# Stick-breaking attention in a two-layer trunk: the short query blocks of two neighbouring pairs of heads computed as one unit

## The chip, the cores and the metric

The kernel runs on one core of one Trainium2 chip. The metric is device time in microseconds (us), from the start of the program to its end. A core has five engines with queues of their own: TensorE (PE), VectorE (DVE), ScalarE (ACT), GpSimd (POOL) and SyncE (SP, which here only starts transfers). Each runs its instructions in the order in which the program has them and waits on semaphores for the others. Matmuls write PSUM, which has eight banks of 512 float32 columns; DVE and ACT read them from there.

## What is computed

One inference step of a decoder trunk with two layers. Layer 0 mixes tokens with a convolution, layer 1 with stick-breaking attention; a gated FFN follows each. There are 512 prompt tokens and 8 x 4 decode tokens with 256 cached keys each. The change touches only the prompt's part of the attention of layer 1:

```
z = einsum('bqhd,bkhd->bhqk', q, k) * HEAD_DIM ** -0.5 + bias      # 16 heads of 64
valid = k_pos < q_pos
log_fail = where(valid, log_sigmoid(-z), 0)
after = cumsum(log_fail, reverse=True) - log_fail
weights = where(valid, exp(log_sigmoid(z) + after), 0)
out = einsum('bhqk,bkhd->bqhd', weights, v)                        # then out @ attn_w_o
```

Queries go in blocks of 128; block i sees the first (i + 1) x 128 keys.

## The kernel before, in words

**Heads and units.** The 16 heads are 8 pairs (`pair(c)`, L2206); the two heads of a pair lie in the two halves of the 128 partitions. A pair's four query blocks need 512, 384, 256 and 128 keys. They are cut into three units (`UNITS`, L2202): block 3 (512 columns), blocks 2 and 0 side by side (384 + 128 = 512 columns), and block 1 (256 columns).

**Steps of a unit** (`unit`, L2210). PE computes the logits of both heads into two PSUM banks (L2221, tag `z`). ACT takes the exponential of each (L2226) into a tile `e`. POOL clears what is not causal (L2233). DVE clamps (L2238). ACT takes the logarithm of 1 + e into a tile `s` (L2240). DVE sums it from the right with a scan for each head and block (L2249). ACT takes exp(-s) (L2253). DVE multiplies e by it (L2254): these are the weights. PE transposes them in squares of 128 (L2261) into the one bank with tag `t`, a head at a time, and ACT copies each head's transposes into a tile `w` (L2264). PE then multiplies them with the values (`products`, L2277) into the one bank with tag `av`.

**Tiles.** There are three `e` and three `w` tiles of 2 x 512 columns, one of each with 2 x 256, and one `s` tile of each size (L80). An `e` tile is free when it is transposed, a `w` tile when its products are done.

**After a pair.** For the first seven pairs ACT copies the result over the pair's queries (L2292); its split into a high and a low part (`XH` by ACT, L2286, and `XL` by DVE, L2287, in `out`) is held out until the last pair is planned. For the last pair the split reads the bank `av` itself, in four pieces of 128 columns.

**Work beside it.** In the same stage PE projects keys and values of all pairs, with float32r matmuls in threes (`weighted`, L1981 to L1983: high x high, high x low, low x high), each operation being six matmuls over two of the eight input chunks. They are the fill. The decode tokens' logits and products (L2101, L2163, L2183) and transposes of pages, keys and values (L2089, L2011) are in between. At the end of the stage the fill is the first four output products (attention result times `attn_w_o`, L2345), into banks `acc`, `z`, `z` and `one`. Each is four operations; the last of each four needs the last two pairs' `XH` and `XL`.

**What sets the order.** Each step is given to a planner (`Plan`, L85) with an engine, an estimated cost, and what it reads and writes. `run` (L170) goes through time: for each engine it takes the ready operation with the lowest key, which is its start less a share of its rank (the longest chain behind it) less `urgent`. `fill` operations come after all others that are ready within 0.15. A matmul of another array shape (`form`: logits use 64 rows, products 64 columns, the decode products 32 columns) than the one before is charged 0.17. The instructions are issued in this order.

**After the stage.** DVE adds the four banks to the residual `xT` (L2361), in the order `acc`, `z`, `z`, `one`. PE goes on with `add_group` (L2368): the same four weight slots for the other 288 token columns, in new banks (L460 to L462). The first of these takes the PSUM bank in which the `acc` product lay, so its first matmul waits for the first add.

Of the kernel before, what the change touches and what calls it, by code (L numbers as in the profile page):

```python
# [13 lines left out]
AF = mybir.ActivationFunctionType  # L14
# [3 lines left out]
P = 128  # L18
# [58 lines left out]

BIG = 1.0e17
AHEAD = 3
E_BUFS, S_BUFS, W_BUFS = (3, 1), (1, 1), (3, 1)  # L80
NEAR, PATIENT = 0.15, 2.0


# [142 lines left out]
def tile_trunk(  # L226
# [207 lines left out]
    def uid(s):  # L434
        _n[0] += 1
        return f"{s}_{_n[0]}"
# [197 lines left out]
    start_cm, start = open_pool("start")  # L634
# [42 lines left out]
    plan = Plan(E_CONV, 0.12)  # L677
# [382 lines left out]
    for c in range(0, NC, 2):  # L1060
# [137 lines left out]
    for h, (c0, n) in enumerate(STREAMS):  # L1198
        if h:
            layer_norm(1)  # L1200
        for g in (0, 4):
            for i in range(4):
                c = g + i
                pt = product(s0 + c, h)
                x = xT[:, c, c0:c0 + n]
# [3 lines left out]
        if not h:  # L1209
# [6 lines left out]
    n = SA[1]  # L1216
    plan.op("pe", 0.53, lambda: pe.matmul(ms()[:, :n], mean_m, nrm.acc[0]()[:, :n], start=True, stop=True),
            r=[nrm.acc[0]], w=[ms])
    plan.op("act", 0.34, lambda: act.activation(rs()[:, :n], ms()[:, :n], AF.Sqrt, bias=eps_t[:, 0:1], scale=1.0),
            r=[ms, "table"], w=[rs])  # L1220
    plan.op("dve", 1.7, lambda: dve.reciprocal(rs()[:, :n], rs()[:, :n]), w=[rs])
    for c in range(NC):
        u = plan.tile("u", NC, lambda: nrm.tile("u", NC))
        e, name, cost = on("pool" if c in POOL_U else "dve", n, 1.05e-3, 2.25e-3)
        plan.op(name, cost, lambda c=c, u=u, e=e: e.tensor_tensor(u()[:, :n], xT[:, c, 0:n], rs()[:, :n], op=ALU.mult),
                r=[rs, ("x", c, 0)], w=[u])
# [4 lines left out]
            r=[u, ("XH", c, 0)], w=[("XL", c, 0)], lift=NLIFT)  # L1231
# [694 lines left out]
    HALF = [slice(0, HD), slice(HD, P)]  # L1926
# [5 lines left out]
    plan = Plan()  # L1932
# [14 lines left out]
    def sbuf(tag, w, bufs, dt=F32, pool_=va):  # L1947
        return plan.tile(tag, bufs, lambda: pool_.tile([P, w], dt, tag=tag, name=uid(tag), bufs=bufs))
# [7 lines left out]
    def dcost(n):  # L1956
        return 0.09 + n * 1.1e-3

    def acost(n):
        return 0.1 + n * 0.95e-3  # L1960
# [238 lines left out]
            r=[t], w=["Zd0", "Zd1"] + [("Zd", i) for i in range(4)])  # L2199


    UNITS = [[(3, 0)], [(2, 0), (0, 3 * P)], [(1, 0)]]  # L2202

    held_out = []

    def pair(c):  # L2206
        b = [bb[:, 2 * c + j:2 * c + j + 1] for j in range(2)]
        av = psum("av")

        def unit(u, parts):  # L2210
            n = sum((i + 1) * P for i, _ in parts)
            z = [psum("z") for _ in range(2)]
            e, s, w = (sbuf(f"{tag}{n}", 2 * n, bufs[n < 512]) for tag, bufs in (("e", E_BUFS), ("s", S_BUFS), ("w", W_BUFS)))

            def two(x):
                return x()[:, :2 * n].rearrange("p (j k) -> p j k", j=2)

            def logits():
                for i, lo in parts:
                    for j in range(2):  # L2220
                        pe.matmul(z[j]()[:, lo:lo + (i + 1) * P], qT[HALF[j], c, i * P:(i + 1) * P],  # L2221
                                  kT[HALF[j], c, 0:(i + 1) * P], start=(lo == 0), stop=True, skip_group_check=True)

            plan.op("pe", 1.69e-3 * n, logits, r=[("q", c), ("k", c, 0), ("k", c, 1)], w=z, form="r64")
            for j in range(2):
                plan.op("act", acost(n), lambda j=j: act.activation(two(e)[:, j, :n], z[j]()[:, :n], AF.Exp, bias=b[j]),  # L2226
                        r=[z[j]], w=[(e, j)])


            def causal():  # L2230
                for i, lo in parts:
# [8 lines left out]
            plan.op("act", acost(2 * n), lambda: act.activation(two(s)[:, :, :n], two(e)[:, :, :n], AF.Ln, bias=1.0),  # L2240
                    r=ej, w=[(s, 0), (s, 1)])

            for j in range(2):
                for i, lo in parts:
# [9 lines left out]
            plan.op("dve", 0.08 + 2 * n * 1.08e-3, lambda: dve.tensor_tensor(  # L2254
                two(e)[:, :, :n], two(e)[:, :, :n], two(s)[:, :, :n], op=ALU.mult), r=sj, w=ej)
            for j in range(2):
                t = psum("t")

                def turn(j=j, t=t):
                    for k in range(n // P):  # L2260
                        pe.transpose(t()[:, k * P:(k + 1) * P], two(e)[:, j, k * P:(k + 1) * P], ident)  # L2261

                plan.op("pe", 0.82e-3 * n, turn, r=[(e, j)], w=[t])
                plan.op("act", acost(n), lambda j=j, t=t: act.copy(two(w)[:, j, :n], t()[:, :n]), r=[t], w=[(w, j)])  # L2264

            return w

        ws = [unit(u, parts) for u, parts in enumerate(UNITS)]

        def products(us, cost, key):  # L2270
            def f():
                for u in us:
                    w = ws[u]
                    for i, lo in UNITS[u]:
                        for kc in range(i + 1):
                            for j in range(2):
                                pe.matmul(av()[HALF[j], i * P:(i + 1) * P], vtok[c % 3][:, kc, HALF[j]],  # L2277
                                          w().rearrange("p (j k) -> p j k", j=2)[:, j, lo + kc * P:lo + (kc + 1) * P],
                                          start=(kc == 0), stop=(kc == i), skip_group_check=True)

            plan.op("pe", cost, f, form="c64", w=[key],
                    r=[*((ws[u], j) for u in us for j in range(2)), ("vtok", c % 3, 0), ("vtok", c % 3, 1)])

        def out(lo, n, src, r, key):
            cols = slice(lo, lo + n)
            plan.op("act", acost(n), lambda: act.copy(XH[:, c, cols], src(cols)), r=r, w=[("XH", c, key)], a=[("X", c)])  # L2286
            plan.op("dve", dcost(n), lambda: dve.tensor_tensor(XL[:, c, cols], src(cols), XH[:, c, cols], op=ALU.subtract),  # L2287
                    r=[*r, ("XH", c, key)], a=[("X", c)])

        if c < NC - 1:  # L2290
            products(range(len(UNITS)), 2.1, av)
            plan.op("act", acost(512), lambda: act.copy(qT[:, c, 0:SEQ], av()), r=[av], w=[("q", c)])  # L2292
            held_out.append(lambda: out(0, SEQ, lambda cols: qT[:, c, cols], [("q", c)], 0))
        else:
            for u in range(len(UNITS)):
                products([u], 0.82e-3 * 2 * sum((i + 1) * P for i, _ in UNITS[u]), (av, u))
            for u in range(len(UNITS)):
                for i, _ in UNITS[u]:
                    out(i * P, P, lambda cols: av()[:, cols], [(av, u)], i)

    def both_halves(f, c):
# [37 lines left out]
    for i, tag in enumerate(("acc", "z", "z", "one")):  # L2339
# [66 lines left out]
```

## Time and profile before

| | |
|---|---|
| median of the runs (lowest, highest) | 1284.79 us (1284.37, 1285.92) |
| profiled execution: its own time | 1284.92 us |
| profiled execution: span | 1283.2 us |
| PE busy in the span | 1267.9 us (99%) |
| DVE busy, ACT busy, POOL busy | 979.9, 713.7, 152.9 us |
| TensorE clock granted, mean | 0.998 |

The span is the time from the first to the last instruction that the profiler recorded; the execution's own time is 1.7 us more. A row of the timeline has the start and the duration of an instruction, both in us, then engine, line, operation, and output <- inputs with their shapes. A number in brackets is the time that the engine sat idle before it, and what ended that. PE overlaps its matmuls: a matmul of 128 x 256 has a row of some 0.28 us, but the next one starts 0.12 us later. So PE is "busy" in the records even where it does less than it can, and what a step takes is read from the distance between starts. [...]

### The profile page before, as it was taken

The numbers are of one execution on the slowest core, as the hardware profiler recorded it, in microseconds if no ns is written. First come the engines' busy times: TensorE is split into PE (matmuls) and PEld (weight loads), VectorE is DVE, ScalarE is ACT, GpSimd is POOL, SyncE is SP. The second block draws the span as 40 slices with busy tenths as digits, with TensorE's granted clock in tenths as the row PEclk, the third lists the DMA queues.
The fourth block names the chain that finished last, engine by engine and source line by source line (L and its number), as shares of the span: only waits on it lengthen the run. The fifth ranks groups of instructions, "written<-read, shape, count | busy, mean of one in ns | idle before, by whom it ended". The sixth has DMA issues, their size and how long they took to land.

```text
span 1283.2 us, 26496 instructions
## 1 busy us (share of the span) xinstructions
PE 1267.9 (99%) x10860; PEld 1213.6 (95%) x10860; DVE 979.9 (76%) x1671; ACT 713.7 (56%) x1440; POOL 152.9 (12%) x289
## 2 busy tenths in 40 slices
PE   9999999999999999999999999999999999999997
PEld 8997799999999999999988988889999999999997
DVE  6899876988987887768366586756988987886864
ACT  7596574645654455445356587754645555454453
POOL 4000014111001000000142123100111011000000
PEclk9999999999999999999999999999999999999999
DMA  8465333123233233144543445333132233232221
GB/s 223 121 181 136 88 100 115 34 84 115 91 108 101 78 106 116 59 142 138 180 152 128 140 133 174 110 117 99 50 101 87 95 117 115 67 111 90 90 76 70
DMA packets 119402, 142.38 MB, mean 111 GB/s; under 512 B 5357, under 2 KB 110469, under 8 KB 119010
## 3 DMA queue, kind: packets, MB, share of 16 engines
q1 hardware_dynamic: 110350, 111.89, 28.2%
q0 software_dynamic: 8640, 28.78, 7.0%
q8 instruction: 85, 1.39, 0.5%
q14 instruction: 35, 0.29, 0.1%
q10 hardware_dynamic: 292, 0.02, 0.0%
HBM read 129.34 MB, written 12.18 MB: 110 GB/s over the span
## 4 chain that ended last, share of the span: by engine, by line
PE 84%; DVE 11%; issue 2%; ACT 1%; DMA 1%; DVEq 0%; SPq 0%; POOL 0%; ACTq 0%; POOLq 0%
PE acc L1557 5%; PE acc L1555 5%; PE acc L1556 5%; PE acc L712 4%; PE acc L713 4%; PE acc L714 3%; PE acc L460 3%; PE acc L462 3%; PE acc L461 3%; PE tr L1557 3%; PE tr L1556 3%; PE tr L1555 3%; PE av L1353 3%; PE acc L1981 3%; PE av L1355 3%; PE av L1354 3%
## 5 line engine op out<-in xcount | busy, mean ns | idle before, releaser
L373 DVE TENSOR_TENSOR wlo<-raw,whi 128x1024 fp32r<-128x1024 f32 (+2 forms) x245 | 257.4, 1052 | 45.5 <-ACT whi L370 43.8
L370 ACT CAST whi<-raw 128x1024 fp32r<-128x1024 f32 (+2 forms) x245 | 223.5, 914 | 117.3 <-PE av L1354 24.6
L712 PE MATMUL acc<-XH,whi 128*128 128x288 f32 (+1 forms) x384 | 114.5, 298 | 0.0
L713 PE MATMUL acc<-XL,whi 128*128 128x288 f32 (+1 forms) x384 | 110.9, 289 | 0.1
L714 PE MATMUL acc<-XH,wlo 128*128 128x288 f32 (+1 forms) x384 | 110.4, 288 | 0.1
L1981 PE MATMUL acc<-XH,whi 128*128 128x256 f32 (+1 forms) x264 | 82.8, 314 | 0.6 <-ACT XH L2286 0.6
L1555 PE MATMUL acc<-TH,whi 128*128 128x272 f32 x288 | 82.9, 288 | 0.0
L1557 PE MATMUL acc<-TH,wlo 128*128 128x272 f32 x288 | 82.8, 288 | 0.0
L1556 PE MATMUL acc<-TL,whi 128*128 128x272 f32 x288 | 82.8, 287 | 0.0
L1591 ACT COPY G<-acc 128x272 f32<-128x272 f32 (+1 forms) x72 | 26.8, 372 | 94.9 <-PE acc L1557 94.9
L1353 PE MATMUL av<-HH,whi 128*128 128x288 f32 x256 | 76.2, 298 | 0.2
L1982 PE MATMUL acc<-XL,whi 128*128 128x256 f32 (+1 forms) x264 | 76.2, 289 | 0.1
L1983 PE MATMUL acc<-XH,wlo 128*128 128x256 f32 (+1 forms) x264 | 75.9, 287 | 0.0
L1354 PE MATMUL av<-HL,whi 128*128 128x288 f32 x256 | 75.5, 295 | 0.0
L1355 PE MATMUL av<-HH,wlo 128*128 128x288 f32 x256 | 75.3, 294 | 0.0
L712 PEld LDWEIGHTS acc<-XH,whi 128*128 128x128 f32 x384 | 72.2, 188 | 2.8 <-issue 1.6
L713 PEld LDWEIGHTS acc<-XL,whi 128*128 128x128 f32 x384 | 72.3, 188 | 1.0 <-DVE XL L964 0.3
L714 PEld LDWEIGHTS acc<-XH,wlo 128*128 128x128 f32 x384 | 72.2, 188 | 0.3 <-DVE wlo L373 0.3
L1354 PE MATMUL tr<-HL,whi 128*128 128x256 f32 x256 | 71.9, 281 | 0.0
L1353 PE MATMUL tr<-HH,whi 128*128 128x256 f32 x256 | 71.9, 281 | 0.0
L1355 PE MATMUL tr<-HH,wlo 128*128 128x256 f32 x256 | 71.5, 279 | 0.0
L1494 DVE SCALAR_TENSOR_TENSOR cv<-G,fprm,cv 128x560 f32<-128x560 f32 x88 | 69.4, 797 | 0.5
(405 smaller groups left out, 4391.8 us busy)
## 6 DMA issues: line engine op xcount, KB each, us to landing
raw<-in_ffn_w_gate_dram SPq DMA_DIRECT2D x22, 1024.0 KB
raw<-in_ffn_w_up_dram SPq DMA_DIRECT2D x22, 1024.0 KB
raw<-in_ffn_w_down_dram SPq DMA_DIRECT2D x24, 768.0 KB
raw<-in_attn_w_qkv_dram SPq DMA_DIRECT2D x12, 1024.0 KB
raw<-in_conv_w_in_dram POOLq DMA_DIRECT2D x6, 1024.0 KB, 7.9
rep<-glu SPq DMA_DIRECT2D x36, 142.0 KB
raw<-in_conv_w_out_dram POOLq DMA_DIRECT2D x4, 1024.0 KB, 5.8
raw<-in_ffn_w_down_dram SPq DMA_DIRECT2D x8, 512.0 KB
```

The lines of the kernel that those rows point to most:

```text
L370: act.copy(hi[:, k, :], src[:, k])
L373: dve.tensor_tensor(lo[:, k, :], src[:, k], hi[:, k, :], op=ALU.subtract)
L712: pe.matmul(o, hi[:, k, :], XH[:, k, c0:c0 + n], start=(k == 0), stop=False)
L713: pe.matmul(o, hi[:, k, :], XL[:, k, c0:c0 + n], start=False, stop=False)
L714: pe.matmul(o, lo[:, k, :], XH[:, k, c0:c0 + n], start=False, stop=(k == NC - 1))
L1353: pe.matmul(o, hi[:, j + k, :], xh, start=(start and k == 0), stop=False, **kw)
L1354: pe.matmul(o, hi[:, j + k, :], xl, start=False, stop=False, **kw)
L1355: pe.matmul(o, lo[:, j + k, :], xh, start=False, stop=(stop and k == len(xs) - 1), **kw)
L1555: pe.matmul(o, hi[:, j + k, :], xh, start=(start and k == 0), stop=False, **kw)
L1556: pe.matmul(o, hi[:, j + k, :], xl, start=False, stop=False, **kw)
L1557: pe.matmul(o, lo[:, j + k, :], xh, start=False, stop=(k == 3), **kw)
L1981: pe.matmul(o, hi[:, k, :], XH[:, k, c0:c0 + n], start=(k == 0), stop=False)
```

## The change

- Block 1 of pairs c and c + 1 (c even) is one unit of 256 + 256 = 512 columns; it is planned with pair c. There are 4 such units in place of 8 with 256 columns, so 20 units in place of 24. Its two exponentials of each head stay apart, since each pair has its own bias, and so do the scans. Clamp, logarithm, exp(-s), multiplication, and the transposes and copy of each head run over 512 columns of each head.
- The copy after the transposes writes back into `e`; the tiles `w` are gone. There are six `e` and two `s` tiles, all of one size. An `e` tile is now held until its products are done.
- The last pair's three products get `urgent` 3.0, where they had none.

```diff
+LAST_AV = 3.0
-E_BUFS, S_BUFS, W_BUFS = (3, 1), (1, 1), (3, 1)
+E_BUFS, S_BUFS = 6, 2
...
-    UNITS = [[(3, 0)], [(2, 0), (0, 3 * P)], [(1, 0)]]
+    UNITS = [[(3, 0)], [(2, 0), (0, 3 * P)]]
+    shared = {}
...
-                plan.op("act", acost(n), lambda j=j: act.activation(two(e)[:, j, :n], z[j]()[:, :n], AF.Exp, bias=b[j]),
-                        r=[z[j]], w=[(e, j)])
+                for cc, (lo, m) in cs.items():
+                    plan.op("act", acost(m), lambda j=j, cc=cc, lo=lo, m=m: act.activation(
+                        two(e)[:, j, lo:lo + m], z[j]()[:, lo:lo + m], AF.Exp, bias=bb[:, 2 * cc + j:2 * cc + j + 1]),
+                            r=[z[j]], w=[(e, j)])
...
-                plan.op("act", acost(n), lambda j=j, t=t: act.copy(two(w)[:, j, :n], t()[:, :n]), r=[t], w=[(w, j)])
-
-            return w
...
+                plan.op("act", acost(n), lambda j=j, t=t: act.copy(two(e)[:, j, :n], t()[:, :n]), r=[t], w=[(e, j)])
+
+            return e
+
+        ws = [unit([(i, lo, c) for i, lo in parts]) for parts in UNITS]
+        if c % 2 == 0:
+            shared[c] = shared[c + 1] = unit([(1, 0, c), (1, 2 * P, c + 1)])
+        ws.append(shared[c])
+        units = [*UNITS, [(1, c % 2 * 2 * P)]]
...
-                products([u], 0.82e-3 * 2 * sum((i + 1) * P for i, _ in UNITS[u]), (av, u))
+                products([u], 0.82e-3 * 2 * sum((i + 1) * P for i, _ in units[u]), (av, u), LAST_AV)
```

The code is five lines longer at L2223 and eleven at L2361, so lines differ: logits L2221 are L2226 after, transposes L2261 are L2268, the copy L2264 is L2271, products L2277 are L2288, the fill L1981 to L1983 is L1982 to L1984, the splits L2286 and L2287 are L2297 and L2298, the adds L2361 are L2372, and L460 is L461.

**How PE's order moves.** Three places matter below. The first is the last pair's products on PE, before. `z`, `acc` and `one` are banks of output products, `av` is the bank of the last pair, `w` are its transposed weights:

```order
L1983 MATMUL z_10551<-XH,wlo_10231 128x256
L2277 MATMUL av_10643<-w_772_10425,vtok_8050 64x128 x8
L2277 MATMUL av_10643<-w_781_10502,vtok_8050 64x128 x8
L2277 MATMUL av_10643<-w_790_10559,vtok_8050 64x128 x4
L1981 MATMUL acc_10531<-XH,whi_9907 128x256
L1982 MATMUL acc_10531<-XL,whi_9907 128x256
L1983 MATMUL acc_10531<-XH,wlo_9908 128x256
```

Behind the products stand 24 matmuls of fill, four operations of six, and all four of them need the last pair's split; ahead of them stand 36 that do not need it.

The same place after, `e` being the tiles that now hold the weights:

```order
L1984 MATMUL z_10495<-XH,wlo_10148 128x256
L2288 MATMUL av_10506<-e_10270,vtok_8050 64x128 x8
L2288 MATMUL av_10506<-e_10336,vtok_8050 64x128 x8
L2288 MATMUL av_10506<-e_10200,vtok_8050 64x128 x4
L2189 MATMUL one_10534<-ident,oacc 128x128 x2
L1982 MATMUL acc_10469<-XH,whi_9830 128x256
L1983 MATMUL acc_10469<-XL,whi_9830 128x256
L1984 MATMUL acc_10469<-XH,wlo_9831 128x256
```

The products have moved ahead: behind them stand 78 matmuls of fill, 6 ahead of them since the last transposes. The first 33 of the 78 need no split of the last pair.

The second place is the end of the stage on PE, before, where the next stage begins with L460:

```order
L1981 MATMUL one_10618<-XH,whi_10386 128x256
L1982 MATMUL one_10618<-XL,whi_10386 128x256
L1983 MATMUL one_10618<-XH,wlo_10387 128x256
L460 MATMUL acc_10729<-XH,whi_9907 128x288
L461 MATMUL acc_10729<-XL,whi_9907 128x288
```

The product that ends last before is `one`; `acc` was the first of the four to end, 18 matmuls earlier.

And after:

```order
L1984 MATMUL z_10495<-XH,wlo_10148 128x256
L1982 MATMUL acc_10469<-XH,whi_9830 128x256
L1983 MATMUL acc_10469<-XL,whi_9830 128x256
L1984 MATMUL acc_10469<-XH,wlo_9831 128x256
L461 MATMUL acc_10657<-XH,whi_9830 128x288
```

Now `acc` ends last, right ahead of the next stage's first matmul, which writes into the same bank.

The third place is a shared unit's logits, after, on PE; the two numbers are the two heads' banks:

```order
L2226 MATMUL z_10177<-kT,qT 128x256
L2226 MATMUL z_10179<-kT,qT 128x256
L2226 MATMUL z_10177<-kT,qT 128x256
L2226 MATMUL z_10179<-kT,qT 128x256
L2120 MATMUL one_10183<-kT_s,Qf 32x32 x16
```

Before, each pair's two such matmuls stand as a group of their own, at eight places; now four stand together, at four places.

More of the change, by code (lines that the diff above doesn't have):

```diff
@@ L2199, in new_values, with unit @@
             r=[t], w=["Zd0", "Zd1"] + [("Zd", i) for i in range(4)])
-    UNITS = [[(3, 0)], [(2, 0), (0, 3 * P)], [(1, 0)]]
+    UNITS = [[(3, 0)], [(2, 0), (0, 3 * P)]]
+    shared = {}
     held_out = []
     def pair(c):
-        b = [bb[:, 2 * c + j:2 * c + j + 1] for j in range(2)]
         av = psum("av")
-        def unit(u, parts):
-            n = sum((i + 1) * P for i, _ in parts)
+        def unit(parts):
+            n = 512
             z = [psum("z") for _ in range(2)]
-            e, s, w = (sbuf(f"{tag}{n}", 2 * n, bufs[n < 512]) for tag, bufs in (("e", E_BUFS), ("s", S_BUFS), ("w", W_BUFS)))
+            e, s = (sbuf(tag, 2 * n, bufs) for tag, bufs in (("e", E_BUFS), ("s", S_BUFS)))
+            cs = {}
+            for i, lo, cc in parts:
+                a, m = cs.get(cc, (lo, 0))
+                cs[cc] = (a, m + (i + 1) * P)
             def two(x):
@@ L2243, in unit @@
             for j in range(2):
-                for i, lo in parts:
+                for i, lo, _ in parts:
                     m = (i + 1) * P
@@ L2263, in unit, with products @@
                 plan.op("pe", 0.82e-3 * n, turn, r=[(e, j)], w=[t])
-                plan.op("act", acost(n), lambda j=j, t=t: act.copy(two(w)[:, j, :n], t()[:, :n]), r=[t], w=[(w, j)])
-            return w
-        ws = [unit(u, parts) for u, parts in enumerate(UNITS)]
-        def products(us, cost, key):
+                plan.op("act", acost(n), lambda j=j, t=t: act.copy(two(e)[:, j, :n], t()[:, :n]), r=[t], w=[(e, j)])
[5 more added lines that the diff above has]
+        units = [*UNITS, [(1, c % 2 * 2 * P)]]
+        def products(us, cost, key, urgent=0.0):
             def f():
@@ L2273, in f @@
                     w = ws[u]
-                    for i, lo in UNITS[u]:
+                    for i, lo in units[u]:
                         for kc in range(i + 1):
@@ L2279, in f @@
                                           start=(kc == 0), stop=(kc == i), skip_group_check=True)
-            plan.op("pe", cost, f, form="c64", w=[key],
+            plan.op("pe", cost, f, form="c64", w=[key], urgent=urgent,
                     r=[*((ws[u], j) for u in us for j in range(2)), ("vtok", c % 3, 0), ("vtok", c % 3, 1)])
@@ L2290, in pair @@
         if c < NC - 1:
-            products(range(len(UNITS)), 2.1, av)
+            products(range(len(units)), 2.1, av)
             plan.op("act", acost(512), lambda: act.copy(qT[:, c, 0:SEQ], av()), r=[av], w=[("q", c)])
@@ L2294, in pair @@
         else:
-            for u in range(len(UNITS)):
-                products([u], 0.82e-3 * 2 * sum((i + 1) * P for i, _ in UNITS[u]), (av, u))
-            for u in range(len(UNITS)):
-                for i, _ in UNITS[u]:
+            for u in range(len(units)):
+                products([u], 0.82e-3 * 2 * sum((i + 1) * P for i, _ in units[u]), (av, u), LAST_AV)
+            for u in range(len(units)):
+                for i, _ in units[u]:
                     out(i * P, P, lambda cols: av()[:, cols], [(av, u)], i)
```

10 lines of the change are left out of this document (5 added, 5 removed).

## The prediction

> **What bounds the kernel now.** I read the page first: 26496 instructions, PE busy nearly everywhere. Then the busy times of the attention stage (start of its first fill matmul to the first L460) beside a stretch behind it that is nothing but back-to-back fill:
>
> ```profile
> span 1283.2 us, 26496 instructions
> 642.83:859.40 216.57, 214.77 (x2111) 187.40 (x2110) 147.41 (x228) 145.88 (x274) 51.85 (x71) 1.00 0.44 141
> 860.00:872.00 12.00, 12.00 (x92) 12.00 (x91) 6.10 (x10) 4.60 (x7) 0.00 (x0) 1.00 0.28 89
> ```
>
> The columns behind the length are busy us of PE, PE's weight loads, DVE, ACT and POOL, then granted clock, DMA share and GB/s. PE is busy for 214.77 of 216.57 us, DVE and ACT for some 147 each, and the clock is full: PE bounds the stage, and a change counts only if it takes distance between PE's starts away. By busy matmul time no more than 216.57 - 214.77 = 1.80 us could be won. The weight loads, 187.40 against 12.00 of 12.00 in the pure stretch, say that more is lost than that.
>
> The Trainium skill ("Perfetto Trace Analysis", Identifying the Most-Contended Engine) says the same of the method: matmul occupancy is a bad measure of what is left because matmuls are pipelined, and the weight loads' share is a better one. By it the ceiling would be 216.57 - 187.40 = 29.17 us, an estimate from these rows; the sum below uses neither ceiling.
>
> So I went to the timeline of PE at the stage's end, then to DVE in the same stretch:
>
> ```profile
> 847.48 0.36 PE L1981 MATMUL z<-XH,whi 128*128 128x256 f32 x1
> ...
> 851.93 1.97 PE L2277 MATMUL av<-w,vtok 128*64 128x128 f32 x32
> 854.59 0.66 PE L2277 MATMUL av<-w,vtok 128*64 128x128 f32 x8 [0.69 <-DVE XL L2287]
> 855.18 0.39 PE L1981 MATMUL acc<-XH,whi 128*128 128x256 f32 x1
> ...
> 856.40 0.39 PE L1981 MATMUL acc<-XH,whi 128*128 128x256 f32 x1 [0.61 <-ACT XH L2286]
> 856.93 0.38 PE L1982 MATMUL acc<-XL,whi 128*128 128x256 f32 x1
> 857.15 0.28 PE L1983 MATMUL acc<-XH,wlo 128*128 128x256 f32 x1
> ...
> 859.28 0.27 PE L1983 MATMUL one<-XH,wlo 128*128 128x256 f32 x1
> 859.40 0.30 PE L460 MATMUL acc<-XH,whi 128*128 128x288 f32 x1
> ```
>
> ```profile
> 854.25 0.29 DVE L2287 TENSOR_TENSOR XL<-av,XH 128x128 fp32r<-128x128 f32 x1 [4.77 <-ACT XH L2286]
> 856.38 0.49 DVE L2287 TENSOR_TENSOR XL<-av,XH 128x128 fp32r<-128x128 f32 x2 [0.33 <-ACT XH L2286]
> 857.47 0.42 DVE L2361 TENSOR_TENSOR xT<-acc,xT 128x256 f32<-128x256 f32 x1 [0.59 <-PE acc L1983]
> ```
>
> From 847.48 to 859.40 PE takes 11.92 us for 60 fill matmuls and one pair's products. The reader should see three holes: the last eight product records wait for a split that reads the same bank (0.69), and the fill behind them waits twice for the split of what they have just made. DVE and ACT have nothing else to do there (DVE idle for 4.77 us). There is fill in plenty, but it has been spent ahead of the products.
>
> **The change, part by part.**
>
> *The last pair's products move ahead.* The pair before it shows its products without a wait:
>
> ```profile
> 834.76 2.40 PE L2277 MATMUL av<-w,vtok 128*64 128x128 f32 x40
> 837.09 0.44 PE L2011 MATMUL one<-ident,vT 128*128 128x128 f32 x2
> ```
>
> They take 837.09 - 834.76 = 2.33 us. The 36 fill matmuls from 847.48 to 851.93 take 4.45, 0.12 each but for the edges; the 24 behind would take 24 x 0.12 = 2.9. Without a wait that is 9.7 us, so 11.92 - 9.7 = 2.2 us are waiting. In the new order all three products stand together, so no split can come between them, and 33 fill matmuls that need no split of this pair stand behind them: 33 x 0.12 = 4.0 us. The split took from the products' end, 855.18, to 856.38 + 0.49 = 856.87, so 1.7 us. DVE still has to make three held-out splits or a weight's low part somewhere there; the cover has 2.3 to spare, and beyond that each microsecond comes back. Term: **-2.2** (0 to -2.2).
>
> *A new wait.* `acc` now ends last, and the next stage's first matmul overwrites its bank, so it waits for the add (before, the add had been done for 859.40 - 857.89 = 1.5 us by then). In the rows above `acc`'s last matmul starts at 857.15, the add 0.32 us later, and takes 0.42. From the end of a DVE step (854.25 + 0.29) to the PE start that it releases (854.59) there are 0.05. So PE starts 0.32 + 0.42 + 0.05 = 0.79 us after the last fill matmul in place of 0.12. Behind it is queued all of the next stage. Term: **+0.7** (+0.4 if the add overlaps better, +1.2 if DVE still has a conversion of 0.4 in its queue).
>
> *Eight short units become four.* The logits, and how PE goes into and out of them:
>
> ```profile
> L2221 PE MATMUL z<-kT,qT 64*128 64x256 f32 x32 | 5.6, 428 | 0.0
> ```
>
> ```profile
> 826.41 1.14 PE L2221 MATMUL z<-kT,qT 64*128 64x384 f32 x8
> 827.47 0.40 PE L1981 MATMUL acc<-XH,whi 128*128 128x288 f32 x1
> ...
> 831.30 0.28 PE L1983 MATMUL acc<-XH,wlo 128*128 128x256 f32 x1
> 831.51 0.70 PE L2221 MATMUL z<-kT,qT 64*128 64x256 f32 x4
> 832.14 0.66 PE L2261 MATMUL t<-ident,e 128*128 128x128 f32 x4
> 832.64 0.38 PE L2130 MATMUL one<-ident,Zw 128*128 128x128 f32 x2
> ...
> 837.37 0.60 PE L2261 MATMUL t<-ident,e 128*128 128x128 f32 x4
> 837.72 0.38 PE L1981 MATMUL acc<-XH,whi 128*128 128x288 f32 x1
> 837.94 0.29 PE L1982 MATMUL acc<-XL,whi 128*128 128x288 f32 x1
> ...
> 843.41 0.38 PE L2261 MATMUL t<-ident,e 128*128 128x128 f32 x2
> 843.55 0.36 PE L1981 MATMUL z<-XH,whi 128*128 128x256 f32 x1
> 843.75 0.28 PE L1982 MATMUL z<-XL,whi 128*128 128x256 f32 x1
> ```
>
> 32 records in fours: eight groups. One takes 832.14 - 831.51 = 0.63 us; a group of 512 columns in two parts, which is the shape of the new unit, takes 827.47 - 826.41 = 1.06. Two for one: 2 x 0.63 - 1.06 = 0.20, four times: 0.8. And each group that goes takes its edges with it: ahead of it the distance is 0.21 (831.30 to 831.51) in place of 0.12, behind it four transposes take 0.50 in place of the 0.35 at 837.37. That is 0.24 for each of four: 1.0; I take 0.9, since some new groups stand beside other changes of shape and share an edge already. Transposes: two take 0.14 and the fill behind them begins with 0.20 in place of 0.12; four take 0.35, then 0.22 in place of 0.13. Two of the first, 2 x 0.22, equal one of the second, 0.44: nothing. Term: **-1.7** (-0.8, the columns alone, to -2.0).
>
> The Trainium skill ("TensorEngine Tiling (Array Packing)", Key Properties) says that a change of tiling mode drains TensorE; the 0.21 and 0.50 beside the logits are such edges, and no row tells a drain from another cause.
>
> *Fewer steps on ACT, DVE.* Two logarithms of a short unit become one of a long:
>
> ```profile
> 832.41 1.06 ACT L2240 ACTIVATE s<-e 128x1024 f32<-128x1024 f32 x1
> 837.17 0.61 ACT L2240 ACTIVATE s<-e 128x512 f32<-128x512 f32 x1
> ```
>
> That is 2 x 0.61 - 1.06 = 0.16 us; four such pairs of ACT steps (logarithm, exponential, two copies) at four units are some 2.6 us of ACT's 145.88, less on DVE. PE's fill hides both engines for most of the stage; I cost this at nothing. It could give something only where PE waits for the chain.
>
> *The chain's length and the tiles.* The last unit planned decides whether PE waits at the end:
>
> ```profile
> 821.45 1.13 PE L2221 MATMUL z<-kT,qT 64*128 64x512 f32 x4
> 837.91 1.22 DVE L2254 TENSOR_TENSOR e<-e,s 128x1024 f32<-128x1024 f32 x1
> 839.41 0.60 PE L2261 MATMUL t<-ident,e 128*128 128x128 f32 x4
> 840.68 0.66 PE L2261 MATMUL t<-ident,e 128*128 128x128 f32 x4 [0.21 <-ACT w L2264]
> 841.47 0.37 PE L1981 MATMUL z<-XH,whi 128*128 128x256 f32 x1
> ```
>
> The last pair's first unit went from logits (821.45) to its first transposes (832.14) in 10.7 us; the 384 + 128 unit from 826.41 to the end of its multiplication (837.91 + 1.22) in 12.7, beside others. In the new order that unit is the last, and between its logits and its transposes PE has 36 fill matmuls (4.6 us), a pair's products (2.5), 14 transposes with edges (about 2.2), its own logits (1.06) and a decode product (0.5): about 11 us. So PE may wait 0 to 1.7 us there. But before had such a wait too: from 839.41 to 841.47 are 12 transposes, 0.9 us of work and 1.1 of waiting. I take the two as equal. Term: **0** (-0.7 to +1.5).
>
> **The sum:** -2.2 + 0.7 - 1.7 + 0 = **-3.2 us**, against the profiled execution's 1284.92: 1281.7. Its time lies 0.13 above the runs' median, so for the median 1281.6. About 0.2%, here 2.6 us, is what a measurement of this kernel tells from no change.
>
> **The rivals.**
>
> *The wait follows the products* (chance 0.27). If the last unit's chain takes its 12.7 us against 11 of cover and the add's wait is 1.0, the sum is -2.2 + 1.0 - 1.7 + 1.0 = -1.9: 1282.9, not to be told from no change. For it: the two lengths above. Against: ACT loses work.
>
> *No wait is left* (0.12). If the old wait of 1.1 us before 841.47 goes, and the add's wait is only 0.4: -2.2 + 0.4 - 1.7 - 0.7 = -4.2, 1280.6.
>
> *The ring of six stalls the pairs: slower* (0.05). An `e` tile is held from its exponential to its products:
>
> ```profile
> 754.69 1.13 PE L2221 MATMUL z<-kT,qT 64*128 64x512 f32 x4
> 773.16 1.13 PE L2221 MATMUL z<-kT,qT 64*128 64x512 f32 x4
> 808.64 1.63 PE L2277 MATMUL av<-w,vtok 128*64 128x128 f32 x25
> ```
>
> A pair passes in 773.16 - 754.69 = 18.5 us, and needs 2.5 tiles, so six tiles allow a hold of 2.4 x 18.5 = 44.3 us. The sixth pair was held from 773.16 to 808.64, 35.5 us. Above 44.3 each microsecond costs 1 / 2.4 = 0.42 per pair, 2.1 over the five pairs from the fourth on; from 47.1 on, the gain and 2.6 us more are gone. At 48 it would be 3.7 x 2.1 = 7.8: 1284.8 - 3.2 + 7.8 = 1289.4. Against: 8.8 us of room.
>
> *It doesn't do what it says.* That the products are not earlier is excluded by the order, which has them ahead of all 78.
>
> **How the numbers follow.** The forecast (-2.6 to -4.0) has 0.56. Faster by over 0.2% come the forecast and the case without a wait: 0.56 + 0.12 = 0.68. Within 0.2% comes the wait that follows: 0.27. Slower comes the ring: 0.05. The range for 8 in 10 takes in the case without a wait, and most of the first rival with the wait at its larger ends: -2.2 + 1.2 - 0.8 + 0.9 = -0.9, so 1283.9; and on the other side -2.2 + 0.4 - 2.0 - 0.7 = -4.5 and 0.4 more for the runs' spread, so 1279.9.
>
> **What would show it.** Right: in the new profile the products of the last pair are followed by fill at 0.12 us from start to start, without a wait for `XH` or `XL`; the first L461 has a wait of 0.5 to 1.0 us for L2372; four groups of logits with 256 columns take 1.06 us each; and the stage from first fill to L461 is some 213.4 us in place of 216.57. Wrong: a wait before the last unit's transposes of more than 2 us; an ACT exponential that waits for products (L2288); or a stage that is shorter while the time is not, which would mean that the next stage waits for its weights.

## The result

| | before | after |
|---|---|---|
| median of the runs (lowest, highest) | 1285.35 us (1284.32, 1286.45) | 1282.36 us (1281.52, 1284.67) |
| profiled execution: its own time | 1284.92 us | 1283.03 us |
| the stage: first fill matmul to the next stage's first matmul | 216.57 us | 214.00 us |
| from there to the span's end | 423.80 us | 423.85 us |

Both kernels ran twelve times beside each other. The ratio is 0.9977 with a 95% interval of 0.9969 to 0.9984: the change makes the kernel faster, by 3.0 us in the medians. The two profiled executions differ by only 1.89 us, because the code ahead of the stage, which is the same in both, happened to end 0.66 us later in the one of after (643.49 against 642.83 us). Behind the stage the two differ by 0.05 us. So the change is in the stage: **-2.57 us**, and 2.57 - 0.66 = 1.91 is the difference of the two executions to 0.02 us.

### The profile page after: what moved, and what is told of

Its sections match the earlier page's. It is cut to its first block, busy times and chain, and to the rows that moved or that the text cites. A ratio compares the mean times of both kernels' runs of the same rounds, so it can differ in the third digit from the quotient of the medians.

```text
span 1281.3 us, 26460 instructions
## 1 busy us (share of the span) xinstructions
PE 1265.2 (99%) x10860; PEld 1213.9 (95%) x10860; DVE 977.5 (76%) x1663; ACT 711.3 (56%) x1424; POOL 156.0 (12%) x289
## 5 line engine op out<-in xcount | busy, mean ns | idle before, releaser
L1982 PE MATMUL acc<-XH,whi 128*128 128x256 f32 (+1 forms) x264 | 82.3, 312 | 0.0
L1983 PE MATMUL acc<-XL,whi 128*128 128x256 f32 (+1 forms) x264 | 76.1, 288 | 0.0
L1984 PE MATMUL acc<-XH,wlo 128*128 128x256 f32 (+1 forms) x264 | 75.9, 287 | 0.0
```

Of the source, the lines that this page charges most:

```text
L1982: pe.matmul(o, hi[:, k, :], XH[:, k, c0:c0 + n], start=(k == 0), stop=False)
```

## The profile after

The page's first line, then the busy times of the stage and of 12 us of pure fill behind it (us, then PE, weight loads, DVE, ACT, POOL, granted clock, DMA share, GB/s):

```profile
span 1281.3 us, 26460 instructions
643.49:857.49 214.00, 212.39 (x2111) 187.50 (x2109) 144.46 (x218) 143.16 (x256) 55.01 (x71) 1.00 0.45 143
858.00:870.00 12.00, 12.00 (x92) 12.00 (x92) 6.84 (x12) 5.05 (x9) 0.00 (x0) 1.00 0.28 89
```

The weight loads' busy time is the same as before (187.40 then, 187.50 now) in a shorter stage: what went is time without a load, while the work that loads stayed. The clock is full in both, so no part of the difference is clock. ACT has 18 records fewer and DVE 10 fewer, some 3 us of busy time each.

PE's timeline at the stage's end answers to the first rows of the prediction:

```profile
844.62 0.28 PE L1984 MATMUL z<-XH,wlo 128*128 128x256 f32 x1
844.83 2.40 PE L2288 MATMUL av<-e,vtok 128*64 128x128 f32 x40
847.16 0.44 PE L2189 MATMUL one<-ident,oacc 128*128 128x128 f32 x2
847.36 0.36 PE L1982 MATMUL acc<-XH,whi 128*128 128x256 f32 x1
847.56 0.28 PE L1983 MATMUL acc<-XL,whi 128*128 128x256 f32 x1
...
851.37 0.28 PE L1982 MATMUL one<-XH,whi 128*128 128x256 f32 x1
...
856.48 0.28 PE L1983 MATMUL acc<-XL,whi 128*128 128x256 f32 x1
856.60 0.28 PE L1984 MATMUL acc<-XH,wlo 128*128 128x256 f32 x1
857.49 0.37 PE L461 MATMUL acc<-XH,whi 128*128 128x288 f32 x1 [0.61 <-DVE xT L2372]
```

And DVE's in the same stretch:

```profile
848.09 0.88 DVE L2298 TENSOR_TENSOR XL<-av,XH 128x128 fp32r<-128x128 f32 x4 [0.55 <-ACT XH L2297]
...
856.92 0.42 DVE L2372 TENSOR_TENSOR xT<-acc,xT 128x256 f32<-128x256 f32 x1 [7.17 <-PE acc L1984]
```

The reader should see two things. The products of the last pair are one row of 40 records again (20 products in the program's order, each shown as two records), 2.33 us from start to start, and no fill behind them carries a bracket: the split ends at 848.09 + 0.88 = 848.97, while the 34th fill matmul, the first that needs it, starts at 851.37. The cover has 2.4 us to spare. And a new hole stands at the very end: 857.49 - 856.60 = 0.89 us in place of 0.12, so 0.77 us of waiting for the add.

All of PE's waits in the stage, grouped by what was waited for (us in total, how often, the longest), after:

```profile
PE acc L461 <- DVE xT L2372: 0.6, 1, 0.6
PE one L2012 <- DVE vtok L2038: 0.6, 1, 0.6
PE one L2012 <- DVE kr L2026: 0.2, 1, 0.2
PE one L2131 <- DVE vtok L2038: 0.2, 1, 0.2
```

before:

```profile
PE av L2277 <- DVE XL L2287: 0.7, 1, 0.7
PE acc L1981 <- ACT XH L2286: 0.6, 1, 0.6
PE t L2261 <- ACT w L2264: 0.2, 1, 0.2
```

The two waits for the last pair's split are gone, the one for the add is there, and waits for `vtok` and `kr` have come in other places. This view counts only time in which PE had no record at all, and PE's records overlap. The distance between starts shows the rest: 0.61 by the bracket is 0.77 by the starts.

The logits with 256 columns, grouped over the stage of after, and one group with the rows beside it:

```profile
L2226 PE MATMUL z<-kT,qT 64*128 64x256 f32 x32 | 4.5, 402 | 0.0
```

```profile
767.39 0.41 PE L2012 MATMUL one<-ident,kT 128*128 128x128 f32 x2 [0.24 <-DVE kr L2026]
767.73 1.14 PE L2226 MATMUL z<-kT,qT 64*128 64x256 f32 x8
```

32 records as before, 4.5 us of busy time in place of 5.6, in four groups; PE's next start lies 1.06 us behind each of them.

A last table holds for all kernels below. It is worked out from the starts of PE's matmuls in the trace: the distance from each start to the next, summed by what the matmul is, so that each line adds up to the stage to 0.02 us (us; "other" is decode work):

```
                          fill  transposes  logits  products  other   stage
before                  117.75     39.67     22.19    19.59   17.37   216.57
after                   117.44     39.23     21.27    18.68   17.37   214.00
values first            116.59     39.64     22.19    18.83   17.46   214.72
merge only              118.12     39.17     21.27    19.59   17.38   215.51
in place only           118.03     38.73     22.16    19.59   17.37   215.89
acc first               116.79     39.23     21.27    18.68   17.38   213.36
ring of 5               117.40     39.15     21.27    18.68   17.39   213.90
ring of 4               118.64     42.50     21.27    19.57   17.30   219.28
6 and 1 tiles           117.95     37.98     21.27    18.83   17.40   213.44
own w: 3, 2, 3          118.28     39.11     22.48    18.83   17.71   216.42
own w: 3, 1, 4          117.46     40.13     21.27    18.83   17.41   215.10
own w: 3, 1, 3          117.04     39.24     21.27    18.83   17.30   213.67
own w: 3, 2, 3, 2.33    116.62     38.87     21.27    18.83   17.74   213.34
acc first, 7 and 1      117.58     37.70     21.27    18.83   17.40   212.78
```

Waits are inside these sums, with the matmul before the wait. Two columns hardly move but for the change's own doing: logits take 22.16 to 22.19 us with three units for each pair and 21.27 with merged ones (one case apart, below), and products 19.6 with the last pair's late and 18.7 to 18.8 with them ahead. Fill and transposes, where the planner puts the rest, move by up to 5 us from kernel to kernel.

## The experiments

Theory: the sum of the prediction, that is the waits at the end go (-2.2), the wait for the add comes (+0.7), the merge shortens logits and edges (-1.7), and the tiles do nothing. Against it stand the rivals of the prediction, and that the tiles, not the merge, gave part of it. All ratios are to the kernel before, run beside each on the same chip.

**Values first alone.** Before, with the last pair's products urgent and nothing else:

```diff
-            plan.op("pe", cost, f, form="c64", w=[key],
+            plan.op("pe", cost, f, form="c64", w=[key], urgent=3.0 if c == NC - 1 else 0.0,
```

> The kernel before with one edit: the last pair's three products get urgent 3.0. Units and tiles stay as before. In PE's order the product that ends last is z, and acc ends six matmuls earlier, so the new wait of 0.77 us measured in the changed kernel should shrink to some 0.1. Theory (terms add up): the waits of 2.2 us around the last pair's products go, so 2.1 us less than before, and the stage from first fill to L460 takes some 214.4 us in place of 216.57. Rival (the gain comes from the merged units alone): 0 to 0.5 us less, stage 216 or more.

1284.28 us, ratio 0.9983 (0.9974 to 0.9992); stage 214.72, so -1.85. What PE still waits for, the whole list:

```profile
PE t L2261 <- ACT w L2264: 0.2, 1, 0.2
```

Both waits at the end are gone, and since `acc` doesn't end last here, none has come.

**The merge alone.** After, with the products' urgency taken back:

```diff
-LAST_AV = 3.0
+LAST_AV = 0.0
```

> The changed kernel with urgent 0.0 for the last pair's products: units merged, weights in the exponentials' tiles. In PE's order 18 + 6 + 12 fill matmuls stand ahead of the products again and 24 behind, as before. Theory (terms add up): only the merge's 1.7 us (0.8 to 2.0) are won, the waits for the last pair's split are there again, stage 214.9 us. Rival (all comes from the products' place): 0 to 0.5 us less than before. Other rival (all comes from the merge): 3 us less, as with the whole change.

1284.89 us, ratio 0.9996 (0.9987 to 1.0005), which is no difference that can be told; stage 215.51, so -1.06. The waits of before's end are back:

```profile
PE av L2288 <- DVE XL L2298: 0.7, 1, 0.7
PE one L2012 <- DVE vtok L2038: 0.6, 1, 0.6
PE acc L1982 <- ACT XH L2297: 0.6, 1, 0.6
PE one L2012 <- DVE kr L2026: 0.2, 1, 0.2
PE one L2131 <- DVE vtok L2038: 0.2, 1, 0.2
```

The three waits for `vtok` and `kr` are the same as in after: they belong to the order that the merge makes. So the stage goes 216.57, 215.51 by the merge, 214.00 by the urgency on top of it: -1.06 and -1.51.

**`acc` first.** After, with an urgency on the last operation of the `acc` product, so that it ends first of the four and its add is done before the next stage overwrites the bank:

```diff
-            last = plan.op("pe", 6 * SA[1] * COL, weighted(pt, o0 + i, 0, q), w=[pt], follows=last,
+            last = plan.op("pe", 6 * SA[1] * COL, weighted(pt, o0 + i, 0, q), w=[pt], follows=last, urgent=3.0 if i == 0 else 0.0,
```

> The changed kernel with one more edit: the four operations of the acc output product get urgent 3.0, so that it is finished 54 matmuls ahead of the next stage's first matmul, which writes its bank. Theory: the wait of PE for the add (0.77 us at the first L461) goes and nothing else changes: 0.7 to 0.8 us less than the changed kernel, 3.7 less than before, stage some 213.3 us. Rival (PE then waits for something else there, a later add or the next weights): the same time as the changed kernel within 0.3 us, with another wait at or behind the first L461.

1281.99 us, ratio 0.9970 (0.9958 to 0.9983); stage 213.36, 0.64 less than after. PE's timeline at its end:

```profile
856.00 0.28 PE L1984 MATMUL z<-XH,wlo 128*128 128x256 f32 x1
856.12 0.29 PE L461 MATMUL acc<-XH,whi 128*128 128x288 f32 x1
```

0.12 us from the last fill to the next stage. So the wait for the add hangs on which bank ends last, and the change left this on the table: 0.64 of the 0.77 us came back.

**The tiles.** In place alone: before with its three units, but the copies write into `e` (six tiles of 512 columns and two of 256, `s` unchanged).

```diff
-E_BUFS, S_BUFS, W_BUFS = (3, 1), (1, 1), (3, 1)
+E_BUFS, S_BUFS = (6, 2), (1, 1)
...
-                plan.op("act", acost(n), lambda j=j, t=t: act.copy(two(w)[:, j, :n], t()[:, :n]), r=[t], w=[(w, j)])
+                plan.op("act", acost(n), lambda j=j, t=t: act.copy(two(e)[:, j, :n], t()[:, :n]), r=[t], w=[(e, j)])
```

> The kernel before, three units for each pair, with one edit: the transposed weights are copied back into the exponentials' tiles, six with 512 columns of each head and two with 256, no w tiles (the same bytes as before). Urgent and merge are not in it. Theory (the tiles cost and bring nothing by themselves in these units; own w tiles hurt the merged units only because the shared unit's w tile is held over two pairs and leaves two for the rest): stage 216.0 to 217.0 us as before, time within 0.5 us of before. Rival (tiles in common let the units run ahead in any case): stage 214 to 215 us, 1.5 to 2.5 us less than before.

1284.54 us, ratio 0.9996 (0.9987 to 1.0005); stage 215.89, -0.68. No difference in the time; the stage is a little shorter, by transposes (38.73 in place of 39.67), in another order.

The other way round, after with tiles `w` of its own, three `e`, two `s` and three `w`:

```diff
-E_BUFS, S_BUFS = 6, 2
+E_BUFS, S_BUFS, W_BUFS = 3, 2, 3
...
-                plan.op("act", acost(n), lambda j=j, t=t: act.copy(two(e)[:, j, :n], t()[:, :n]), r=[t], w=[(e, j)])
+                plan.op("act", acost(n), lambda j=j, t=t: act.copy(two(w)[:, j, :n], t()[:, :n]), r=[t], w=[(w, j)])
```

> The changed kernel with weights in tiles of their own again: three e and three w tiles of 2 x 512 columns in place of six e, two s. Merge and urgent stay. In PE's order acc ends six matmuls ahead of the next stage, so the wait for the add is some 0.1. Theory (the tiles do nothing, only the three terms count): -2.2 - 1.7 + 0.1, that is 3.6 to 3.9 us less than before. Rival (writing into the same tile is what lets the units run ahead): 1 to 2 us less than before, with waits of ACT or PE for a tile in the middle of the stage.

1284.76 us, ratio 0.9994 (0.9985 to 1.0003); stage 216.42: the gain is gone. "The tiles do nothing" seemed to have fallen. The first explanation was that a shared unit's `w` tile is held over two pairs, so that three are too few. Four of them (and one `s`, as many bytes as the change has) should give it back, three with one `s` should not. Both are the diff above with other numbers, `3, 1, 4` and `3, 1, 3`:

> The changed kernel, but the transposes are copied into tiles of their own again: three tiles for the exponentials, four for the weights, one for the logarithms (as many bytes as the change has). The version with three, three and two of them had a stage of 216.42 us where the change has 214.00. Theory: a shared unit's weight tile is held from its copy to the products of the second of its two pairs, so of three such tiles one is gone for most of the time; a fourth gives it back, and the stage is 213.4 to 214.8 us, the time 0.9975 to 0.9987 of before. Rival: what counts is that six tiles serve both uses, as they are needed; then four and three are short as well and the stage is 215.5 or more, the time 0.999 or more of before.

> The kernel beside it with three weight tiles in place of four (three for the exponentials, one for the logarithms). It tells whether the fourth weight tile or the second tile of logarithms made the difference. Theory (the held weight tile): the stage stays at 215.5 to 216.8 us, 1.5 us or more above the one with four weight tiles, and the time is within 0.001 of before. Rival (the second tile of logarithms did the harm, the third weight tile suffices): the stage is within 0.7 us of the one with four.

Four: 1283.61 us, 0.9988 (0.9979 to 0.9997), stage 215.10. Three: 1282.37 us, 0.9981 (0.9972 to 0.9990), stage 213.67. The kernel with fewer tiles is the one with the shorter stage, so the held tile explains nothing. The rows of PE and ACT where the first version (3, 2, 3) loses most in one place show what does. PE:

```profile
732.19 1.71 PE L2226 MATMUL z<-kT,qT 64*128 64x256 f32 x8
734.29 0.38 PE L1982 MATMUL acc<-XH,whi 128*128 128x256 f32 x1 [0.40 <-ACT kT L2020]
```

ACT:

```profile
731.43 1.28 ACT L2232 ACTIVATE e<-z,bb 128x512 f32<-128x512 f32 x2
732.68 0.63 ACT L1918 ACTIVATE xT<-xT 128x512 f32<-128x512 f32 x1
733.35 0.63 ACT L1919 ACTIVATE xT<-xT 128x512 f32<-128x512 f32 x1
733.88 0.35 ACT L2020 COPY kT<-acc 128x256 f32<-128x256 f32 x1
```

No tile is waited for; three PSUM banks are. From the logits' start to PE's next row there are 2.10 us in place of 1.06. The two exponentials of another unit end at 732.14 and 732.71, and each frees a bank `z` in which PE's logits of one head start 0.05 us later, at 732.19 and 732.77. By the starts inside the row this costs 0.57 us. The copy of 0.35 us that frees PE's bank `acc` stands behind these and two more steps on ACT, and PE's next instruction is fill into that bank: 0.47 us more. That is the odd 22.48 in the table. If such places come and go with the order, then the same tiles and the same instructions in another order must give another stage. The last experiment is this version with one estimate of the planner changed, a pair's products at 2.33 us, as measured, in place of 2.1:

```diff
-            products(range(len(units)), 2.1, av)
+            products(range(len(units)), 2.33, av)
```

> The version with weight tiles of their own (three, two and three), whose stage was 216.42 us, with nothing changed but one estimate that the planner works with: a pair's products are put down at 2.33 us, as measured, in place of 2.1. The instructions and the tiles are the same, their order is not. Theory (the 2.4 us that this version lost to the change were not the tiles' doing but waits of PE that one order has and another has not): the stage ends somewhere else between 213.0 and 215.6 us, with other waits, the time 0.9965 to 0.9988 of before. Rival (that set of tiles is short, whatever the order): the stage stays at 215.9 to 217 us and the time within 0.001 of before.

1281.84 us, ratio 0.9976 (0.9967 to 0.9985); stage 213.34: 3.08 us shorter than with the other estimate, and no longer than the change's. Its waits are two:

```profile
PE one L2050 <- DVE vtok L2038: 0.9, 1, 0.9
PE t L2268 <- ACT w L2271: 0.3, 1, 0.3
```

So the tiles have no price that these runs show; the order that the planner happens to find has one, of some 3 us in these two.

**How many tiles are too few.** After with five and with four shared tiles (`E_BUFS` 5, 4):

> The changed kernel with five e tiles in place of six. Ring rival of the prediction: the hold allowed falls from 44.3 to 2.0 x 18.5 = 37 us, still above the 35.5 of the sixth pair, so nothing. Theory (a hold is no fixed length: logits are only issued later, and the chain needs some 13 us and the products): stage 213.5 to 214.5 us. The rival with a fixed hold that has grown by the merge (over 37 us): 2 us more for each microsecond, 216 us or more.

> The changed kernel with four e tiles. Ring rival with a fixed hold of 35.5 us: the limit is 1.6 x 18.5 = 29.6 us, so 5.9 x 2.1 = 12 us more, stage 226 us. Theory (the hold shrinks with the ring): a loss only where the last pair's chain becomes the last thing, since its tiles come free late and in PE's order only 24 matmuls of fill stand behind its products again: 2 to 4 us more than the changed kernel, stage 216 to 218 us.

Five: 1283.67 us, 0.9985 (0.9976 to 0.9995), stage 213.90, which is 0.10 from the change. Four: 1288.18 us, 1.0022 (1.0013 to 1.0032), stage 219.28. ACT's waits for the products that free a tile, with five:

```profile
ACT e L2232 <- PE av L2288: 0.8, 2, 0.5
```

with four:

```profile
ACT e L2232 <- PE av L2288: 2.5, 5, 0.7
```

The change with six has no such line; with four, five exponentials wait for products. The ring's stall is real, but two tiles further down than feared. PE itself doesn't wait for these exponentials. Its own list of waits with four begins:

```profile
PE t L2090 <- ACT kT L2094: 0.8, 2, 0.5
PE t L2268 <- ACT e L2271: 0.8, 2, 0.5
```

By the starts PE loses some 2.7 us between 668 and 689 us, ahead of transposes whose bank `t` a copy must free first; after loses 0.1 there. And the last pair's products stand in two groups again, at 848.47 and 856.89, with a wait of 0.5 us inside and waits of 0.5 us for the split behind them. The loss of 5.28 us against the change is more than the 2 to 4 expected; how much of it is the ring's own and how much the order's is open.

**One `s` tile.** After with `E_BUFS, S_BUFS = 6, 1`:

> The changed kernel with one s tile in place of two (before there were one long and one short). Theory (the s tile is held only from logarithm to multiplication, some 6 us of a unit's chain, and 20 units need 120 of 217 us): little, stage 214 to 215.5 us. Rival (two s tiles are what lets two units' chains overlap): 2 us or more, with PE waiting for DVE's multiplication or ACT's exponentials in the middle of the stage.

1281.95 us, ratio 0.9978 (0.9967 to 0.9988), stage 213.44. In its order `one` ends last, and the wait for the add (0.77) doesn't arise, which is more than the 0.56 that its stage gains; the second `s` tile buys nothing that shows.

**A version made from these.** After with `acc` first, seven shared tiles and one `s` (`E_BUFS, S_BUFS = 7, 1`):

> The changed kernel with the last four matmul operations in the other order (acc first, so that the add of its bank is done before the next stage overwrites it, worth 0.64 us alone) and seven shared tiles with one for the logarithms in place of six and two. Theory: the ring of six does not stall anything, so a seventh tile gives nothing itself, and the gains are those of acc first (0.64 us) and of fewer changes of tiled shape, 30 entries in place of 34 at some 0.2 us: stage 214.0 - 0.6 - 0.8 = 212.6 us, with 0.4 for waits that come or go elsewhere; time 0.9960 to 0.9974 of before. Rival: an entry costs nothing of its own and the differences so far were waits; then the stage is 213.2 to 213.6 us, as with acc first alone, the time 0.997 to 0.998.

1282.02 us, ratio 0.9977 (0.9967 to 0.9988), stage 212.78, the shortest of all and 1.22 less than the change's; its time can't be told from the change's. Its only wait by the list is 0.5 us for `vT`. The stage lies nearer to the 212.6 of the theory than to the rival's 213.2 to 213.6. But taking where starts lie further apart than such rows usually do, PE is held up for some 1.6 us in `acc` first (0.40 at `kr`, 0.32 and 0.77 at `vtok`, 0.13 ahead of a page's transposes) and for some 1.0 us here (0.62 at `vT`, the rest in pieces under 0.15), so waits alone can account for the 0.58 us that it gains on `acc` first, as the rival has it. The table gives changes of tiled shape no clear price either: products and logits cost nearly the same, and fill takes 0.79 us more where transposes take 1.53 less. What an entry costs by itself stays open.

## Why the prediction was right, and where its sizes were off

The forecast was the likeliest case, 1281.6 us; 1282.36 was measured, inside the range. The mechanisms came as put, and the sum was too large by 0.6 us: -3.2 against -2.57 in the stage. That the medians show -3.0, nearer to the sum, is luck: the interval of the ratio is some 1.9 us wide, and the median of before had been 1284.79 where it is 1285.35 here.

*The last pair's products ahead: -2.2.* Right in mechanism and size. From merge only to after the products' column falls by 0.91, and fill by 0.68 although the wait for the add (0.77) came in: 0.91 + 0.68 + 0.77 = 2.36, less the 0.06 that transposes give back: 2.3. Values first alone gave -1.85 net, since the order moved elsewhere too. The cover had the spare 2.4 us that the prediction gave as 2.3.

*The wait for the add: +0.7.* Right: +0.77, and 0.64 comes back when `acc` ends first. The add started 856.92 - 856.60 = 0.32 us behind the last fill's start and took 0.42, both as taken. PE began 0.15 us after its end (856.92 + 0.42 = 857.34 to 857.49), not 0.05: the step was priced by a split's release of PE, and that 0.10 is the whole miss.

*The merge: -1.7.* This is the term that was mis-sized: the merge alone gave -1.06. The columns were put at 0.8, and the logits' column shows 0.92, of which 0.11 is a wait behind one of before's eight groups. The edges were put at 0.9, as if each group that goes took one entry and one exit of 0.24 with it. In PE's order the number of entries into a tiled shape (logits, products, decode logits and products) from the full one fell from 36 to 34, not by four, since the remaining groups lost neighbours with which they had shared an edge, and the merge's order has its own waits at fill (by the starts 0.39 for `kr`, 0.32 for `vtok` and 0.13 ahead of a page's transposes; before had 0.24 and 0.15). Fill and transposes together show 157.42 before and 157.29 with the merge alone: -0.13 net, where the prediction had -0.9. The waits at fill are 0.45 of the difference, so the edges themselves gave about 0.5, and the new order's waits took most of it back. The prediction treated the rest of the order as fixed; the planner redraws it.

*ACT, DVE and tiles: nothing.* Not contradicted. No run takes ACT's 2.7 us and DVE's 3.0 us less of busy time apart from the merge, and the terms above leave nothing for them. The same tiles of their own (3, 2, 3) give 213.34 or 216.42 by order alone.

*The last unit's chain: 0.* Right as a balance (0.8 us of waiting in both), in another place than thought. Before's old wait was read too large: transposes in a row start 0.11 us apart, and the fill behind them 0.03 us after the last, so the 12 from 839.41 to 841.47 are 1.2 us of work, not 0.9, and 0.8 of waiting, not 1.1. After has no wait ahead of its last units' transposes, but one between the value transposes (PE, then DVE):

```profile
835.77 0.38 PE L2012 MATMUL one<-ident,vT 128*128 128x128 f32 x2
836.76 0.41 PE L2012 MATMUL one<-ident,vT 128*128 128x128 f32 x2 [0.61 <-DVE vtok L2038]
837.01 0.63 PE L2268 MATMUL t<-ident,e 128*128 128x128 f32 x4
837.57 2.40 PE L2288 MATMUL av<-e,vtok 128*64 128x128 f32 x40
```

```profile
835.00 1.22 DVE L2261 TENSOR_TENSOR e<-e,s 128x1024 f32<-128x1024 f32 x1
836.19 0.42 DVE L2038 COPY vtok<-one 128x256 f32<-128x256 f32 x1
```

A copy of 0.42 us stands behind a multiplication of 1.22. 836.76 - 835.77 = 0.99 us, 0.77 more than two transposes take.

*The rivals.* The wait that follows the products would have left waits of 1 us ahead of the last unit's transposes, and none stands there. "No wait is left" did not come in after; `acc` first is that case in part. The ring: its limit of 44.3 us scales to 37.0 for five tiles and 29.6 for four (2.0 and 1.6 times 18.5), and with a hold of 35.5 it says that five suffice and four don't. Both came so, but its price was far too high: (35.5 - 29.6) / 1.6 for each of five pairs would be 18 us (12 in the expectation, by the factor for six tiles), and 5.3 were lost against the change. The step that failed there is that one pair stood for all, in both numbers. The hold: from a pair's first logits to its products after takes 20.2 us (last pair) to 67.9 us (second). With four tiles the sixth pair's rows are

```profile
783.04 1.13 PE L2226 MATMUL z<-kT,qT 64*128 64x512 f32 x4
...
819.48 2.40 PE L2288 MATMUL av<-e,vtok 128*64 128x128 f32 x40
```

so 36.4 us, where after has 32.5. But the second, third and fourth pair shrank from 67.9, 66.3 and 54.4 us to 58.3, 52.3 and 32.3. The interval: before's first and last pair begin at

```profile
652.37 1.13 PE L2221 MATMUL z<-kT,qT 64*128 64x512 f32 x4
...
821.45 1.13 PE L2221 MATMUL z<-kT,qT 64*128 64x512 f32 x4
```

and 169.08 / 7 = 24.2 us lie between pairs on the mean, from 15.8 to 41.5 singly. So taking a tile away moves the pairs as well as stalling them, and no limit worked out from one hold and one interval gives the price; the runs with five and four tiles do.

## What to carry to other kernels

Where a planner sets the order, price a change by the terms that can be seen in the rows (here the logits' columns, 0.9 us, and the waits at the stage's end, 2.2), and give the rest a spread: the same instructions in the same tiles ended 3 us apart because one estimate had changed. So don't read a loss after such a change as the fault of the resource that was touched before the same resource has been tried in a second order. And when the order of the last products moves, look at which bank the next stage writes first: let that one end first.

## What the runs showed that was not expected

- The time of one execution hides a change of this size. In the fourteen profiled executions the same code ahead of the stage ended anywhere from 642.10 to 644.93 us, a spread of 2.8 us that is larger than the change's effect, while behind the stage it took 423.75 to 424.47. The stage's length leaves both out. No kernel was profiled twice, so how well a whole stage repeats is not shown; the three waits for the last pair's split, which before, merge only and in place only share, agree to 0.01 us by the starts.
- A wait of PE costs more than its bracket says: 0.61 us of idle time was 0.77 us by the starts, at the add and at `vtok` alike, and 0.40 was 0.47 at the fill behind the logits of the version with own tiles. Inside that row of logits 0.57 us were lost without any bracket.
